# Two output projections of a decoder trunk, rewritten as one level of Strassen's scheme

## The chip, the cores and the metric

One core of a Trainium2 chip runs the whole kernel. The metric is the device time of one execution in microseconds (us). The kernel before has a median of 1701.39 us in three runs (1700.16 to 1702.24).

## The reference

A decoder trunk of two layers on 512 tokens of 2048 features, all in float32. Each layer computes `y`, multiplies it by an output weight of 2048 x 2048, and normalizes the sum with its input:

```
def even_layer(x, w_in, conv_w, cmp_pos, cmp_w1, cmp_w2, w_out, rel_table):
    ...
    return jnp.concatenate([y_a, y_b], axis=-1) @ w_out
def odd_layer(x, w_in, ln_g, ln_b, sgu_w, sgu_b, w_out):
    ...
    y = u * mixed.reshape(bsz, s, D_SGU) * jax.nn.silu(z)
    return y @ w_out
def reference(...):
    for layer in range(DEPTH):
        ...
        x = layer_norm(DEEPNORM_ALPHA * x + y, ln_g[layer], ln_b[layer])
    return x
```

The change concerns the two products with `w_out` and the additions and LayerNorms behind them.

## The kernel before

**Numbers.** A float32 product is made of three products of fp32r parts: `split` (lines 80 to 82) casts a tile to its high part on ScalarE and subtracts that from the tile on VectorE for the low part. Then hi·hi, lo·hi and hi·lo are added up in one PSUM bank. Weights pass through `split` in halves of 128x1024 (`whi`, `wlo`), from a raw buffer of 1 MB that SP's queue loads; activations are split once (`act_hi`, `act_lo`).

**Stages.** The even layer makes its features with feature-major units and attention heads and writes `y_sb` (features on partitions, 512 tokens). Output projection 1 multiplies by `wo0`. Its blocks are token-major: `proj_blocks` goes over column blocks of 512, 512, 512, 256 and 256 columns, `block_b` keeps one PSUM bank for each of the four row tiles of 128 tokens ("rows" below), and `mm_b` issues the three matmuls of one 128-deep piece (lines 113 to 115). In the last block each row is finished before the next row begins. `done0` loads the piece of x (`xs`), adds it to the bank into `xr`, and takes bn_stats; behind a row's last block `layer_norm` normalizes the row. VectorE does 1408 of its 2048 columns (lines 502 and 512), ScalarE and GpSimd the other 640 (lines 507 to 509), with the reciprocal root on GpSimd (line 498). `transposes0` (line 529) then turns row m-2 into `act_hi` and `act_lo`, and the last two rows are turned between the first blocks of the odd layer's projection (`wv1`).

**The odd layer** makes `v_sb` by that projection, then loops over 16 column tiles (units of `wuz`, the spatial mix into `pm`, line 601, and the gate, lines 597 to 607), and writes its `y` back into `v_sb`. Output projection 2 multiplies it by `wo1` in the same blocks; `done1` (line 614) adds, normalizes and stores rows.

**Order.** There is no table. A framework's scheduler orders each engine's instructions by the program's order and the buffers' dependences. SP issues the loads into one queue; each engine works through its own list in order.

## Time and profile before

| what | value |
|---|---|
| runs, median (lowest to highest) | 1701.39 us (1700.16 to 1702.24) |
| span of the profiled execution | 1699.9 us |
| TensorE busy | 1668.3 us, 98% |
| VectorE busy | 704.3 us, 41% |
| ScalarE busy | 464.1 us, 27% |
| GpSimd busy | 59.2 us, 3% |
| TensorE on the chain that ended last | 95% |
| mean granted clock of TensorE | 0.993 |

The span runs from the first to the last instruction of the profiled execution; no other time is listed for that execution, and the median of the runs is 1.5 us above it. The chain is followed back from the last instruction: a share of 95% says that TensorE waits for little. The busy time of matmuls overlaps, since their ends are modelled: what one matmul costs is read from the distance between two starts.

### The profile page before, as it was taken

The page shows a single profiled execution, that of the slowest core. Times are in us where ns is not written, and L with a number is a line of the kernel's source. Part 1 is how long each engine was busy: PE and PEld are TensorE (multiplying, and loading weights), DVE is VectorE, ACT ScalarE, POOL GpSimd, SP SyncE. Part 2 cuts the span into 40 slices and gives each one's busy share as a digit, 9 for nine tenths or more (in the row PEclk, how much of TensorE's full clock was granted, in tenths as well). Part 3 has the DMA queues.
Part 4 walks back from the last instruction along what each step waited for, and adds up shares of the span by engine and source line. Part 5 has one row for each costly group of instructions (what it writes and reads, how often), then busy time and mean ns, then how long its engine had stood idle before and what let it go on. Part 6 is the DMA issues. An engine that isn't in the chain of part 4 may idle for free.

```text
span 1699.9 us, 19851 instructions
## 1 busy us (share of the span) xinstructions
PE 1668.3 (98%) x8390; PEld 1423.9 (84%) x8390; DVE 704.3 (41%) x1161; ACT 464.1 (27%) x717; POOL 59.2 (3%) x96
## 2 busy tenths in 40 slices
PE   8999999999999999999999899999999999999995
PEld 6898888888988888888889898888888888888895
DVE  5225353444244435354334932233333333353337
ACT  4123232333232323243111422222222222241111
POOL 0100000000000000000000500000000000000004
PEclk9999999999999999999999999999999999999998
DMA  6542222222222222223334222222222222232222
GB/s 225 174 157 100 104 81 75 106 74 80 102 100 81 76 105 75 75 99 136 124 124 134 80 100 99 99 75 99 99 99 84 90 99 99 88 135 99 99 75 99
DMA packets 32244, 175.44 MB, mean 103 GB/s; under 512 B 4211, under 2 KB 7155, under 8 KB 13980
## 3 DMA queue, kind: packets, MB, share of 16 engines
q1 hardware_dynamic: 31340, 171.13, 28.4%
q0 software_dynamic: 672, 2.64, 0.5%
q8 instruction: 65, 1.06, 0.3%
q10 hardware_dynamic: 144, 0.41, 0.1%
q14 instruction: 23, 0.19, 0.0%
HBM read 169.95 MB, written 6.84 MB: 104 GB/s over the span
## 4 chain that ended last, share of the span: by engine, by line
PE 95%; DVE 2%; POOL 1%; issue 1%; DMA 0%; ACT 0%; SPq 0%; DVEq 0%; POOLq 0%
PE ps L106 18%; PE ps L104 18%; PE ps L105 18%; PE ps L115 11%; PE ps L114 11%; PE ps L113 11%; PE ps_t L377 1%; PE pm L601 1%; PE hp L271 1%; DVE xr L512 1%; PE po L320 1%; PE po L322 1%; PE po L321 1%; POOL rs L498 0%; PE ps_s L320 0%
## 5 line engine op out<-in xcount | busy, mean ns | idle before, releaser
L82 DVE TENSOR_TENSOR wlo<-raw,whi 128x1024 fp32r<-128x1024 f32 (+3 forms) x286 | 343.2, 1203 | 803.7 <-ACT whi L81 736.0
L81 ACT CAST whi<-raw 128x1024 fp32r<-128x1024 f32 (+3 forms) x286 | 295.0, 1035 | 1080.5 <-PE ps L105 575.5
L104 PE MATMUL ps<-act_hi,whi 128*128 128x512 f32 x1376 | 540.5, 393 | 0.0
L106 PE MATMUL ps<-act_hi,wlo 128*128 128x512 f32 x1376 | 536.0, 390 | 0.7 <-DVE wlo L82 0.7
L105 PE MATMUL ps<-act_lo,whi 128*128 128x512 f32 x1376 | 535.7, 389 | 0.0
L113 PE MATMUL ps<-whi,act_hi 128*128 128x512 f32 (+2 forms) x1088 | 371.0, 341 | 3.1 <-ACT act_hi L81 3.1
L114 PE MATMUL ps<-wlo,act_hi 128*128 128x512 f32 (+2 forms) x1088 | 370.7, 341 | 1.7 <-DVE wlo L82 1.7
L115 PE MATMUL ps<-whi,act_lo 128*128 128x512 f32 (+2 forms) x1088 | 370.6, 341 | 1.4 <-DVE act_lo L82 1.4
L106 PEld LDWEIGHTS ps<-act_hi,wlo 128*128 128x128 f32 x1376 | 258.3, 188 | 55.4 <-DVE wlo L82 1.1
L104 PEld LDWEIGHTS ps<-act_hi,whi 128*128 128x128 f32 x1376 | 258.5, 188 | 52.5 <-issue 0.7
L105 PEld LDWEIGHTS ps<-act_lo,whi 128*128 128x128 f32 x1376 | 258.5, 188 | 51.9 <-issue 0.2
L113 PEld LDWEIGHTS ps<-whi,act_hi 128*128 128x128 f32 x1088 | 207.0, 190 | 25.8 <-ACT act_hi L81 3.3
L114 PEld LDWEIGHTS ps<-wlo,act_hi 128*128 128x128 f32 x1088 | 206.9, 190 | 24.4 <-DVE wlo L82 2.0
L115 PEld LDWEIGHTS ps<-whi,act_lo 128*128 128x128 f32 x1088 | 206.8, 190 | 24.2 <-DVE act_lo L82 1.6
L358 ACT ACTIVATE t_sc<-t_sc,mx 128x128 f32<-128x128 f32 (+1 forms) x64 | 35.1, 550 | 17.0 <-DVE mx L355 17.0
L498 POOL TENSOR_TENSOR rs<-mv,epst 128x1 f32<-128x1 f32 x8 | 8.1, 1008 | 864.3 <-DVE mv L496 864.3
L82 DVE TENSOR_TENSOR p_lo<-ps_t,p_hi 128x512 fp32r<-128x512 f32 (+2 forms) x48 | 25.0, 549 | 0.5
L353 DVE CUSTOM_DVE_ANT_0 t_sc<-ps_s,bh 128x128 f32<-128x128 f32 (+3 forms) x56 | 24.3, 455 | 0.6
L507 ACT ACTIVATE xr<-xr,nm,rs 128x320 f32<-128x320 f32 (+1 forms) x15 | 9.2, 655 | 50.2 <-DVE nm L504 50.2
L364 DVE TENSOR_SCALAR t_sc<-t_sc,sm 128x128 f32<-128x128 f32 (+1 forms) x64 | 20.5, 382 | 0.6
L173 PE MATMUL ps<-act_hi,whi 128*128 128x512 f32 x32 | 13.9, 445 | 6.5 <-ACT act_hi L81 6.2
L377 PE MATMUL ps_t<-ident,t_sc 128*128 128x128 f32 x160 | 20.1, 273 | 0.0
(163 smaller groups left out, 881.9 us busy)
## 6 DMA issues: line engine op xcount, KB each, us to landing
raw<-in_wa_dram SPq DMA_DIRECT2D x54, 1024.0 KB, 4.8
raw<-in_wo_dram SPq DMA_DIRECT2D x32, 1024.0 KB, 4.8
raw<-in_wuz_dram SPq DMA_DIRECT2D x32, 1024.0 KB, 4.8
raw<-in_wv_dram SPq DMA_DIRECT2D x16, 1024.0 KB, 4.8
raw<-in_cw_dram SPq DMA_DIRECT2D x4, 1024.0 KB, 4.8
xraw<-in_xT_dram SPq DMA_DIRECT2D x7, 512.0 KB, 9.7
xs<-in_xn_dram SPq DMA_DIRECT2D x12, 256.0 KB, 3.4
raw<-in_wv_dram SPq DMA_DIRECT2D x4, 670.0 KB, 4.2
```

The source lines that it names most:

```text
L81: nc.scalar.copy(hi, src)
L82: nc.vector.tensor_tensor(lo, src, hi.bitcast(F32), ALU.subtract)
L104: nc.tensor.matmul(ps, hi[:, w], act_hi[:, kt, :], start=kt == 0, stop=False)
L105: nc.tensor.matmul(ps, hi[:, w], act_lo[:, kt, :], start=False, stop=False)
L106: nc.tensor.matmul(ps, lo[:, w], act_hi[:, kt, :], start=False, stop=kt == KT - 1)
L113: nc.tensor.matmul(ps[:, :width], act_hi[:, kt, ms], hi[:, w], start=kt == 0, stop=False)
L114: nc.tensor.matmul(ps[:, :width], act_hi[:, kt, ms], lo[:, w], start=False, stop=False)
L115: nc.tensor.matmul(ps[:, :width], act_lo[:, kt, ms], hi[:, w], start=False, stop=kt == KT - 1)
L353: nc.vector.tensor_tensor_reduce(out=t[:, offs[qb] + k0:offs[qb] + k1], in0=b[:, o:o + k1 - k0], in1=bh[:, BW - nk + k0:BW - nk + k1], sca ...
L358: nc.scalar.activation(t[:, offs[qb]:offs[qb] + nk], t[:, offs[qb]:offs[qb] + nk], AF.Exp, bias=mx[:, qb:qb + 1], accum_out=sm[:, qb:qb + 1])
L364: nc.vector.tensor_scalar(t[:, offs[qb]:offs[qb] + nk], t[:, offs[qb]:offs[qb] + nk], sm[:, qb:qb + 1], None, ALU.mult)
L377: nc.tensor.transpose(ps[:, i * P:(i + 1) * P], t[:, offs[qb] + kb * P:offs[qb] + (kb + 1) * P], ident)
```

## The change

Both projections become `strassen`. `y` and `w_out` are cut into halves by depth (k), by tokens (t) and, within each of two column groups of 1024 (g), by columns (n). Seven products of sums of quarters, in the order 1, 2, 5, 3, 7, 6, 4, take the place of eight. Each has 2 depth pieces (c) x 2 column groups x 2 row tiles x 4 depth tiles x 3 parts = 96 matmuls of 128x512, in units of 24 on one weight megabyte. The sums of activations are made by VectorE in `s_piece`. The sums of weights are made by DMAs: products 1 and 3 load four buffers `ch` of 1 MB each (SP, line 564), and for products 5, 7, 6 and 4 a DMA issued by GpSimd adds a further megabyte of the weight to the buffer (line 568), 16 of them in each projection. Product 2 uses the old raw buffers (line 561).

The sum over products is kept in `xr`: `stage` loads all of x into it (line 632, 4 x 1 MB) and the LayerNorm's gains and biases into `gb` (line 521, 2 x 1 MB) ahead of the weights, and each finished bank is added to one quarter by VectorE (line 581). Product 6 goes into all of three quarters by way of `ua`. Rows 0 and 1 are complete with product 6, rows 2 and 3 with product 4; `layer_norm` follows in each case. The scale of x is moved into `y` (YSCALE) and epsilon (LEPS). All transposes stand behind the first projection in the program. The pools change: `act_hi` and `act_lo` are given up before each projection and `ch` lies in their place; `xr` lies where tiles of the even layer lay, and the second `gb` where tiles of the odd layer's loop lay.

In the changed kernel `split` is at lines 86 and 87, the Strassen matmuls at lines 600 to 602, LayerNorm at lines 497 to 514, bn_stats at line 638 and the transposes at line 659.

```diff
+YSCALE = 0.5 / ALPHA
+LEPS = EPS / ALPHA ** 2
...
-BLOCKS = [(0, 512), (512, 512), (1024, 512), (1536, 256), (1792, 256)]
+BLOCKS = [(0, 512), (512, 512), (1024, 512), (1536, 512)]
...
-    act_hi = big.tile([P, KT, S], F32R, name="act_hi")
-    act_lo = big.tile([P, KT, S], F32R, name="act_lo")
+    act_hi = ea.tile([P, KT, S], F32R, name="act_hi")
+    act_lo = ea.tile([P, KT, S], F32R, name="act_lo")
...
-            nc.vector.scalar_tensor_tensor(y_sb[:, h, :], ah, 0.5, az, ALU.mult, ALU.mult)
+            nc.vector.scalar_tensor_tensor(y_sb[:, h, :], ah, YSCALE, az, ALU.mult, ALU.mult)
...
+    even.close()
+
+
+    xp = ctx.enter_context(tc.tile_pool(name="xp", bufs=1, side="right"))
     xr = xp.tile([P, NT, DM], F32, name="xr")
...
-    for kt in range(KT):
-        split(act_hi[:, kt, :], act_lo[:, kt, :], y_sb[:, kt, :])
...
+    def strassen(sp, w, y, half_done):
...
+        def a(k, t, c):
+            return y[:, 8 * k + 4 * c:8 * k + 4 * c + 4, t * 256:(t + 1) * 256]
+
+        def blk(k, n, g, c):
+            return w[4 * (2 * g + n) + 2 * k + c]
...
+        def s_piece(p, c):
+            if p == 5 and c == 0:
+                for d in range(2):
+                    f1[d] = sp.tile([P, 4, 256], F32, tag="f1", name="f1", bufs=2)
+                    nc.vector.tensor_tensor(f1[d], a(0, 1, d), a(1, 1, d), ALU.subtract)
+            if p == 3 and c == 0:
+                for d in range(2):
+                    nc.vector.tensor_tensor(a(0, 1, d), a(0, 0, d), a(0, 1, d), ALU.subtract)
+                    nc.vector.tensor_tensor(a(0, 0, d), f1[d], a(0, 0, d), ALU.subtract)
+                    nc.vector.tensor_tensor(a(1, 0, d), a(1, 0, d), a(0, 0, d), ALU.add)
+            src = {1: a(0, 0, c), 2: a(1, 0, c), 5: f1.get(c), 3: a(1, 0, c), 7: a(0, 1, c), 6: a(0, 0, c), 4: a(1, 1, c)}[p]
+            hi = sp.tile([P, 4, 256], F32R, tag="shi", name="shi", bufs=3)
+            lo = sp.tile([P, 4, 256], F32R, tag="slo", name="slo", bufs=3)
+            split(hi, lo, src)
+            return hi, lo
+
+        def t_parts(p, g, c):
+            if p == 2:
+                raw = wp.tile([P, 2048], F32, tag="raw", name="raw", bufs=2)
+                nc.sync.dma_start(raw, blk(1, 0, g, c))
+            elif p in (1, 3):
+                raw = chain[g, c] = sp.tile([P, 2048], F32, tag="ch", name="ch", bufs=4)
+                nc.sync.dma_start(raw, blk(0, 0, g, c) if p == 1 else blk(1, 1, g, c))
+            else:
+                raw = chain[g, c]
+                add = {5: (0, 1), 7: (0, 1), 6: (0, 0), 4: (1, 0)}[p]
+                nc.gpsimd.dma_start(raw, blk(*add, g, c), accum_op=ALU.add)
...
+                split(hi, lo, raw[:, d * 1024:(d + 1) * 1024])
...
+        for p in (1, 2, 5, 3, 7, 6, 4):
+            new = p in (1, 5, 7, 6)
+            for c in range(2):
+                shi, slo = s_piece(p, c)
+                for g in range(2):
+                    parts = t_parts(p, g, c)
+                    for m in range(2):
...
+                            nc.tensor.matmul(b, shi[:, k, ms], hi[:, ws], start=new and first, stop=False, **kw)
+                            nc.tensor.matmul(b, shi[:, k, ms], lo[:, ws], start=False, stop=False, **kw)
+                            nc.tensor.matmul(b, slo[:, k, ms], hi[:, ws], start=False, stop=last, **kw)
+                        if c == 0:
+                            continue
...
+                        elif p == 2:
+                            add(at(0, m, g, 0), b)
+                            half_done(m, 2 * g)
...
+                        elif p == 6:
+                            add(ua[g, m], b)
+                            add(at(0, m, g, 1), ua[g, m], ALU.subtract)
+                            half_done(m, 2 * g + 1)
+                            add(at(1, m, g, 1), ua[g, m], ALU.subtract)
+                            half_done(2 + m, 2 * g + 1)
+                            add(at(1, m, g, 0), ua[g, m])
+                        else:
+                            add(at(1, m, g, 0), b)
+                            half_done(2 + m, 2 * g)
+
+    def stage(sp, gbp, w, y, src, stats, g, finish):
+
+        if src is not None:
+            for m in range(NT):
+                nc.sync.dma_start(xr[:, m], src[m * P:(m + 1) * P])
+        gb = gbp.tile([P, 2, DM], F32, tag="gb", name="gb")
+        affine_rows(gb, g)
+        left = [4] * NT
+
+        def half_done(m, b):
+            nc.vector.bn_stats(stats[:, m, b], xr[:, m, b * 512:(b + 1) * 512])
+            left[m] -= 1
+            if not left[m]:
+                finish(m, gb)
+
+        strassen(sp, w, y, half_done)
...
+        stage(sp, gbp, wo0, y_sb, xn, stats0, 2, lambda m, gb: layer_norm(xr, gb, stats0, m, LNS))
...
-    proj_blocks(wo0, BLOCKS, done0)
+    for m in range(NT):
+        transposes0(m)
...
-        vdone.append((m, b))
-        if len(vdone) < 3:
-            transposes0(NT - 3 + len(vdone))
...
-    proj_blocks(wo1, BLOCKS, done1)
...
+        stage(sp, gbp, wo1, v_sb.rearrange("p k n c -> p k (n c)"), None, stats1, 0, out_rows)

```

**SP at the start of projection 1.** SP's queue before (raw is a weight megabyte, xs a piece of x, gb the gains and biases):

```order
L87 DMA raw<-in_wa_dram 128x2048 x11
L87 DMA raw<-in_wo_dram 128x2048 x4
L534 DMA xs<-in_xn_dram 128x512 x2
L519 DMA gb_5692<-in_odg_dram 128x2048 x2
L87 DMA raw<-in_wo_dram 128x2048 x3
L534 DMA xs<-in_xn_dram 128x512 x4
```

The same place now (xr is all of x, ch a weight megabyte of product 1):

```order
L92 DMA raw<-in_wa_dram 128x2048 x11
L561 DMA raw<-in_wo_dram 128x2048 x2
L632 DMA xr<-in_xn_dram 128x2048 x4
L521 DMA gb<-in_odg_dram 128x2048 x2
L564 DMA ch<-in_wo_dram 128x2048 x4
L561 DMA raw<-in_wo_dram 128x2048 x2
L92 DMA raw<-in_wv_dram 128x2048 x2
```

Before, four weight megabytes were issued ahead of x and the gains; now two megabytes of product 2 are, and six megabytes (xr and gb) stand ahead of the first weight of product 1. In the second projection there is no xr, and two megabytes (gb) stand ahead.

**VectorE where the first LayerNorm begins.** Before, in the last block of projection 1 (wlo is the low part of a weight, xr the rows):

```order
L82 TENSOR_TENSOR wlo<-raw,whi 128x1024
L539 SCALAR_TENSOR_TENSOR xr<-xs,ps 128x256
L540 BN_STATS stats_5687<-xr 128x6
L495 BN_AGGR mv<-stats_5687 128x2
L496 TENSOR_SCALAR mv<-mv 128x1
L502 SCALAR_TENSOR_TENSOR xr<-xr,mv,gb_5692 128x512
L504 TENSOR_SCALAR nm<-mv,rs 128x1
L502 SCALAR_TENSOR_TENSOR xr<-xr,mv,gb_5692 128x512
L502 SCALAR_TENSOR_TENSOR xr<-xr,mv,gb_5692 128x384
L512 SCALAR_TENSOR_TENSOR xr<-xr,rs,gb_5692 128x512 x2
L512 SCALAR_TENSOR_TENSOR xr<-xr,rs,gb_5692 128x384
```

Now, from the end of product 6 (ua is a bank of product 6, the first wlo the first half weight of product 4):

```order
L581 TENSOR_TENSOR ua<-ua,ps 128x512
L87 TENSOR_TENSOR wlo<-ch,whi 128x1024
L581 TENSOR_TENSOR xr<-xr,ua 128x512 x2
L638 BN_STATS stats_5656<-xr 128x6 x2
L581 TENSOR_TENSOR xr<-xr,ua 128x512
L581 TENSOR_TENSOR ua<-ua,ps 128x512 x2
L581 TENSOR_TENSOR xr<-xr,ua 128x512 x2
L638 BN_STATS stats_5656<-xr 128x6 x2
```

and on, after the LayerNorm of row 0 and the statistics of row 1:

```order
L581 TENSOR_TENSOR xr<-xr,ua 128x512
L498 TENSOR_SCALAR mv<-mv 128x1
L504 SCALAR_TENSOR_TENSOR xr<-xr,mv,gb 128x512
L506 TENSOR_SCALAR nm<-mv,rs 128x1
L504 SCALAR_TENSOR_TENSOR xr<-xr,mv,gb 128x512
L504 SCALAR_TENSOR_TENSOR xr<-xr,mv,gb 128x384
L514 SCALAR_TENSOR_TENSOR xr<-xr,rs,gb 128x512 x2
L514 SCALAR_TENSOR_TENSOR xr<-xr,rs,gb 128x384
L87 TENSOR_TENSOR wlo<-ch,whi 128x1024 x7
```

Before, the low part of the weight stood ahead of a row's LayerNorm, and one row followed. Now product 4's first half weight stands early, and the other seven behind all of product 6's additions and the LayerNorms of rows 0 and 1. In the second projection VectorE's list is the same at this place.

**TensorE at the same place** (product 4's matmuls, lines 600 to 602; line 659 are the transposes of row 0):

```order
L600 MATMUL ps<-whi,shi 128x512
L601 MATMUL ps<-wlo,shi 128x512
L602 MATMUL ps<-whi,slo 128x512
L600 MATMUL ps<-whi,shi 128x512 x3
L659 MATMUL ps_x<-ident,xr 128x128 x16
L601 MATMUL ps<-wlo,shi 128x512
L602 MATMUL ps<-whi,slo 128x512
L600 MATMUL ps<-whi,shi 128x512
```

Of product 4 16 matmuls stand ahead of the transposes of row 0, and the next (L601) uses the first of the seven late wlo. The other 48 transposes, of rows 1 to 3, stand behind product 4 and ahead of the first matmul of `wv1`; before, those of the last two rows stood between the blocks of `wv1`.

## Rows read from the trace of the kernel before

**Rows 1.** The page: the span; busy time, share and instructions of TensorE.

```profile
span 1699.9 us, 19851 instructions
PE 1668.3 (98%) x8390; PEld 1423.9 (84%) x8390; DVE 704.3 (41%) x1161; ACT 464.1 (27%) x717; POOL 59.2 (3%) x96
```

**Rows 2.** Groups by line and shape: the projections' matmuls (out<-in xcount | busy, mean ns | idle before).

```profile
L113 PE MATMUL ps<-whi,act_hi 128*128 128x512 f32 x576 | 224.3, 389 | 0.0
...
L113 PE MATMUL ps<-whi,act_hi 128*128 128x256 f32 x384 | 110.0, 286 | 3.1 <-ACT act_hi L81 3.1
```

**Rows 3.** Timeline of PE at the start of the second projection: start, duration.

```profile
1505.52 0.48 PE L113 MATMUL ps<-whi,act_hi 128*128 128x512 f32 x1
1505.83 0.40 PE L114 MATMUL ps<-wlo,act_hi 128*128 128x512 f32 x1
...
1508.79 0.39 PE L115 MATMUL ps<-whi,act_lo 128*128 128x512 f32 x1
```

**Rows 4.** Timeline of PE in a 256-wide block of the first projection.

```profile
924.62 0.28 PE L113 MATMUL ps<-whi,act_hi 128*128 128x256 f32 x1
...
925.46 0.28 PE L114 MATMUL ps<-wlo,act_hi 128*128 128x256 f32 x1
```

**Rows 5.** Busy time by stretch, at the first LayerNorm: window, span, engines, PEclk, DMA share, GB/s.

```profile
950.00:960.00 10.00, 5.17 (x32) 4.67 (x31) 10.00 (x15) 6.46 (x10) 4.67 (x4) 0.76 0.06 7
960.00:968.00 8.00, 6.57 (x49) 6.36 (x48) 7.56 (x12) 3.21 (x6) 5.69 (x5) 0.88 0.30 125
```

**Rows 6.** The chain of waits: start-up, start of projection 1, transposes.

```profile
12.79 0.54 PE ps L174
...
16.69 0.24 PE ps L175
...
771.87 0.24 PE ps L113
...
968.94 0.55 PE ps_x L529 x5
```

**Rows 7.** Timeline of DVE: the last operation of the even layer.

```profile
773.43 0.68 DVE L469 SCALAR_TENSOR_TENSOR y_sb<-ah,az 128x512 f32<-128x512 f32 x1
```

**Rows 8.** Busy time by stretch, at the start, with the DMA queue full.

```profile
10.00:15.00 5.00, 3.54 (x10) 2.15 (x9) 4.28 (x4) 3.90 (x4) 0.00 (x0) 0.81 1.03 417
20.00:25.00 5.00, 5.00 (x24) 4.14 (x23) 3.79 (x4) 2.24 (x3) 0.00 (x0) 1.00 0.96 370
```

**Rows 9.** DMA issues: operation, xcount, KB each, us from issue to landing.

```profile
raw<-in_wo_dram SPq DMA_DIRECT2D x32, 1024.0 KB, 4.8
...
rscr<-rrow POOLq DMA_DIRECT2D x8, 320.0 KB, 8.4
...
gb<-in_odg_dram SPq DMA_DIRECT2D x2, 1024.0 KB, 8.6
```

**Rows 10.** Groups by line and shape: VectorE and ScalarE operations that return in the changed kernel.

```profile
L82 DVE TENSOR_TENSOR wlo<-raw,whi 128x1024 fp32r<-128x1024 f32 x270 | 329.8, 1224 | 756.2 <-ACT whi L81 688.4 <-PE pm L601 63.1 <-PE ps_t L377 4.2
L81 ACT CAST whi<-raw 128x1024 fp32r<-128x1024 f32 x270 | 283.2, 1052 | 1032.9 <-PE ps L105 556.7 <-PE ps L115 358.2 <-issue 66.6
...
L607 DVE TENSOR_TENSOR v_sb<-ug,th 128x512 f32<-128x512 f32 x16 | 11.1, 692 | 0.6
...
L82 DVE TENSOR_TENSOR act_lo<-ps_x,act_hi 128x512 fp32r<-128x512 f32 x16 | 10.0, 670 | 0.1
...
L617 DVE SCALAR_TENSOR_TENSOR xr<-xr,ps 128x512 f32<-128x512 f32 x12 | 7.9, 680 | 0.4
...
L618 DVE BATCH_NORM_STATS2 stats<-xr 128x6 f32<-128x512 f32 x12 | 7.7, 682 | 0.0
```

**Rows 11.** Timeline of DVE: LayerNorm of row 2 in the second projection, then row 3.

```profile
1681.16 0.29 DVE L495 BATCH_NORM_AGGREGATE mv<-stats 128x2 f32<-128x30 f32 x1
...
1687.73 0.41 DVE L617 SCALAR_TENSOR_TENSOR xr<-xr,ps 128x256 f32<-128x256 f32 x1
```

**Rows 12.** Timeline of ACT at the end of the odd layer's loop.

```profile
1505.70 0.59 ACT L597 ACTIVATE th<-ps 128x512 f32<-128x512 f32 x1
```

More of the change, by code (lines that the diff above doesn't have):

```diff
@@ L70, in trunk @@
     wp = ctx.enter_context(tc.tile_pool(name="wp", bufs=2))
+    even = ExitStack()
+    ea = even.enter_context(tc.tile_pool(name="ea", bufs=1))
     psp = ctx.enter_context(tc.tile_pool(name="psp", bufs=8, space=PS))
@@ L519, in affine_rows, with at, add @@
             nc.sync.dma_start(gb[:, i], odg[g + i:g + i + 1].to_broadcast([P, DM]))
-    gb0 = lp.tile([P, 2, DM], F32, name="gb0", bufs=1)
+    def strassen(sp, w, y, half_done):
[3 more added lines that the diff above has]
+            return w[4 * (2 * g + n) + 2 * k + c]
+        f1 = {}
+        chain = {}
+        ua = {}
+        def s_piece(p, c):
[24 more added lines that the diff above has]
+                nc.gpsimd.dma_start(raw, blk(*add, g, c), accum_op=ALU.add)
+            parts = []
+            for d in range(2):
+                hi = wp.tile([P, 1024], F32R, tag="hi", name="whi", bufs=4)
+                lo = wp.tile([P, 1024], F32R, tag="lo", name="wlo", bufs=4)
+                split(hi, lo, raw[:, d * 1024:(d + 1) * 1024])
+                parts.append((hi, lo))
+            return parts
+        def at(t, m, g, n):
+            return xr[:, 2 * t + m, (2 * g + n) * 512:(2 * g + n + 1) * 512]
+        def add(dst, src, op=ALU.add):
+            nc.vector.tensor_tensor(dst, dst, src, op)
+        banks = {}
+        for p in (1, 2, 5, 3, 7, 6, 4):
[5 more added lines that the diff above has]
+                    for m in range(2):
+                        if new and c == 0:
+                            banks[g, m, p] = bank()
+                        b = banks[g, m, {2: 1, 3: 5, 4: 7}.get(p, p)]
+                        ms = slice(m * P, m * P + P)
+                        for k in range(4):
+                            hi, lo = parts[k // 2]
+                            ws = slice(k % 2 * 512, k % 2 * 512 + 512)
+                            first, last = c == 0 and k == 0, c == 1 and k == 3
+                            kw = {} if new else {"skip_group_check": True}
+                            nc.tensor.matmul(b, shi[:, k, ms], hi[:, ws], start=new and first, stop=False, **kw)
[3 more added lines that the diff above has]
+                            continue
+                        if p == 1:
+                            ua[g, m] = sp.tile([P, 512], F32, tag="ua", name="ua", bufs=4)
+                            nc.scalar.copy(ua[g, m], b)
+                        elif p == 2:
+                            add(at(0, m, g, 0), b)
+                            half_done(m, 2 * g)
+                        elif p == 5:
+                            add(at(1, m, g, 1), b)
+                        elif p == 3:
+                            add(at(0, m, g, 1), b)
+                        elif p == 7:
+                            add(at(1, m, g, 1), b, ALU.subtract)
+                        elif p == 6:
[8 more added lines that the diff above has]
+                            half_done(2 + m, 2 * g)
@@ L607, in trunk, with out_rows @@
             nc.vector.tensor_tensor(v_sb[:, j].rearrange("p n c -> p (n c)"), ug, th, ALU.mult)
-    for kt in range(KT):
-        split(act_hi[:, kt, :], act_lo[:, kt, :], v_sb[:, kt].rearrange("p n c -> p (n c)"))
-    gl = big.tile([P, 2, DM], F32, tag="big0", name="gl")
-    def done1(m, c0, width, ps):
-        b = BLOCKS.index((c0, width))
-        dst = xr[:, m, c0:c0 + width]
-        nc.vector.scalar_tensor_tensor(dst, dst, ALPHA, ps[:, :width], ALU.mult, ALU.add)
-        nc.vector.bn_stats(stats1[:, m, b], dst)
-        if b == 1 and m == 0:
-            affine_rows(gl, 0)
-        if c0 + width == DM:
-            layer_norm(xr, gl, stats1, m, LNE if m == NT - 1 else LNS, lambda n, cs: (nc.scalar if n % 2 and m == NT - 1 else nc.sync).dma_start(out[m * P:(m + 1) * P, cs], xr[:, m, cs]))
-    proj_blocks(wo1, BLOCKS, done1)
+    odd.close()
+    def out_rows(m, gb):
+        layer_norm(xr, gb, stats1, m, LNE if m == NT - 1 else LNS, lambda n, cs: (nc.scalar if n % 2 and m == NT - 1 else nc.sync).dma_start(out[m * P:(m + 1) * P, cs], xr[:, m, cs]))
+    with tc.tile_pool(name="sp1", bufs=1) as sp, tc.tile_pool(name="gb1", bufs=1, side="right") as gbp:
+        stage(sp, gbp, wo1, v_sb.rearrange("p k n c -> p k (n c)"), None, stats1, 0, out_rows)
 def t5_bucket(n):
```

35 lines of the change are left out of this document (11 added, 24 removed).

## The prediction

> **What bounds the kernel now.** I read the page first: TensorE is busy 1668.3 of 1699.9 us [rows 1], and nearly the whole chain that ended last lies on it. So a matmul taken away is worth its distance to the next, and any wait that is put in front of TensorE costs its full length. Next I read the groups by line and shape for the number of matmuls, and TensorE's timeline for their distance. The mean of 389 ns in the group [rows 2] is a modelled length and overlaps the next matmul; the starts are the measure. In the second projection 14 starts run from 1505.83 to 1508.79 [rows 3]: 2.96 / 13 = 0.228 us for a matmul of 512 columns. In a 256-wide block 8 starts run from 924.62 to 925.46 [rows 4]: 0.84 / 7 = 0.120 us. Then I looked for stretches in which TensorE does wait, since the change could close or open such holes. The one large hole is the first LayerNorm: in 950 to 968 us TensorE is busy 5.17 + 6.57 of 18 us [rows 5], so 6.3 us are idle there. The starts of both projections have no hole: the first matmul of projection 1 is on the chain at 771.87 [rows 6], that of projection 2 starts at 1505.52 [rows 3].
>
> **What the change takes away.** Line 113 has 576 matmuls of 512 and 384 of 256 columns [rows 2] for three projections, so one projection has, over its three lines, 576 and 384 too: 576 x 0.228 + 384 x 0.120 = 177.4 us. Now it has 7 x 96 = 672 of 512 columns: 153.2 us. That is **-24.2 us each, -48.4 together**. The old hole goes too, **-6.3**, and with it one restart of the clock. What a restart costs is seen at the start of the kernel: after its wait TensorE's granted clock is 0.81 in 10 to 15 us [rows 8], and the nine distances from 12.79 to 16.69 [rows 6] take 3.90 us in place of 9 x 0.228 = 2.05: 1.8 us lost while the clock goes from its lower level to 2.4 GHz. At the old hole the clock fell to 0.76 [rows 5], so I take **-1.8**.
>
> **The start of projection 1.** The first weight of product 1 is the seventh megabyte in SP's queue, behind four of xr and two of gb, and xr's memory was the even layer's, so its loads wait for the last y_sb, which ends at 773.43 + 0.68 = 774.1 [rows 7]. Before, the weights were loaded ahead and xs and gb beside the matmuls. Seven times 1.05 MB is 7.34 MB. With a full queue the core moved 417 and 370 GB/s [rows 8]; at 400 that is 18.4 us. A lone megabyte takes 4.8 us from issue to landing [rows 9], of which 2.6 are transfer at that rate, so 2.2 are a start. Then ScalarE casts the first half, 1.05 us [rows 10]. So 774.1 + 2.2 + 18.4 + 1.1 = 795.8, against a TensorE that is done with the even layer at 771.9: **+23.9**. The two megabytes of product 2 that were prefetched don't help, since product 1 comes first. Bounds: 417 or 370 GB/s give 17.6 or 19.8 us of transfer; a gb megabyte took 8.6 us [rows 9], and if two of them cost that each, 12 us more.
>
> **From product 6 to product 4.** VectorE now has, from the end of the first bank of product 6 to the second half weight of product 4: four additions to ua at 0.68, twelve to xr at 0.69, eight bn_stats at 0.68, two low parts at 1.22 [rows 10], and the LayerNorms of rows 0 and 1. One LayerNorm with its aggregation takes VectorE from 1681.16 to 1687.73 [rows 11], 6.57 us, a wait for GpSimd included. The sum is 2.7 + 8.3 + 5.5 + 2.4 + 13.1 = 32.0 us. The first bank is ready 36 matmuls (8.2 us) before the end of product 6, so that half weight is ready 23.8 us after it. TensorE has 16 matmuls, 3.6 us, in front of the one that needs it: it is idle for 20.2 us. In projection 1 the 16 transposes of row 0 lie in this time; five take 0.55 us [rows 6], so 1.8: **+18.4** there. In projection 2 the order is the same without transposes: **+20.2**. Before, a half weight was split ahead of a row's LayerNorm, and one row followed at a time.
>
> **From product 4 to the odd layer.** The first matmul of wv1 stands behind the 48 transposes of rows 1 to 3, which want LayerNorm row 3 and free banks. Product 4's last bank of row 2 is ready 12 matmuls (2.7 us) before its end. VectorE adds and takes statistics (1.4) and does row 2 (6.57): 5.2 us after the end. Then come row 3's addition and statistics (1.4), three splits of transposed rows (2.0) [rows 10] and row 3's LayerNorm: 15.2 us. Some seven of the 13 splits left, at 0.67, then free the banks for the last transposes: 19.9 us, of which 48 x 0.11 = 5.3 are transposes that were there before: **+14.6**. The two weight splits for wv1 stand behind all 13, so I add **+1** for a second short wait.
>
> **The start of projection 2.** Its gb takes memory of the odd layer's loop and waits for the last gate. TensorE ends the loop at 1505.5 [rows 3]; one activation (0.59 [rows 12]) and four VectorE operations of 0.69 [rows 10] later, at about 1508.9, SP may issue. Three megabytes at 400 GB/s take 7.9 us, with 2.2 and 1.1 around them: 1520.1, so **+14.6**.
>
> **Restarts and the end.** Five new holes of over 10 us bring five restarts at 1.8: **+9.0**. At the end the last addition and statistics work on 512 in place of 256 columns: **+0.5**.
>
> **Edits at nothing.** GpSimd's 32 DMA issues stand on an engine that was busy 59.2 us [rows 1]. VectorE's sums of activations and low parts come to some 22 us in the fullest of the middle products (eight low parts of weights, two of activations, six sums at 1.22 and four additions at 0.68: 22.2), about the 96 x 0.228 = 21.9 us of TensorE beside them; with the lighter products around it that costs under 1 us.
>
> **The weight sums.** No row of before shows an accumulating DMA. It is hidden as long as a megabyte takes no more than the 24 matmuls on it, 5.47 us. From below it is a plain copy, 2.6 us at the full rate; from above I take the row of GpSimd's own queue, 8.4 us from issue to landing [rows 9], as the time of one megabyte. A gain is excluded, as the copy alone is needed at least. I take it as hidden, since the queue rows of a weight megabyte (4.8, of which a part is start) are nearest in size. The Trainium skill, "Collectives: The Full Stack", section "The bandwidth ceiling: the fold count and why AG ≠ RS ≠ AR", says that a DMA that adds reads two sources, with two read descriptors for each chunk on one ring, and so runs at half the rate of a copy; as an estimate by that, two times 2.6 is 5.2 us, under 5.47 by little, and at 370 GB/s it would be 5.7, which adds 24 x 0.2 = 5 us. No run here shows it yet.
>
> **The sum.** -48.4 - 6.3 - 1.8 + 23.9 + 18.4 + 20.2 + 14.6 + 1 + 14.6 + 9.0 + 0.5 = +45.7 us on the span of 1699.9. The median of the runs is 1.5 above the span, so the same on it: **1747 us**, slower by 2.7%.
>
> **The rivals.**
> - *The weight sums fall behind.* For it: 4 in 7 products hang on them, one after another on one queue, each on the buffer of the sum before. Against it: they can start a product early. It decides from 5.47 us per megabyte. At 8.4 us, 12 sums in each projection (the first four have a product's time in hand) lose 2.9 each: 2 x 12 x 2.9 = 70 us, 1817.
> - *VectorE does not hold TensorE*, and the change is **faster**. The place is between products 6 and 4 and behind 4. For it: VectorE is busy 41% on the whole, so it might start these additions early and finish them in time. It decides when the 32.0 us of work are under 8.2 + 3.6 = 11.8. Then 18.4, 20.2, 14.6, 1 and three restarts (5.4) go: 45.7 - 59.6 = -13.9, so 1687. Against it: the order on VectorE is fixed, and the durations are rows.
> - *The starts cost nothing*, because the loads of xr and gb are early or give way to the first weight. Then 23.9, 14.6 and two restarts go: +3.6, so 1705. Against it: the loads stand ahead in SP's one queue, and xr's memory is not free earlier.
> - That the change doesn't make seven products is out: the lists have 672 matmuls a projection.
>
> **How the numbers follow.** The forecast gets 0.66, the weight sums 0.22, the free VectorE 0.06 and the free starts 0.06. The forecast's own range is 1730 (restarts at nothing, VectorE's work a tenth shorter) to 1771 (both gb loads slow, 24 us). The range reaches on into the case of slow sums, to 1810, and down to 1715 for a start that is half hidden. A measurement of this kernel can tell about 0.2%, 3.4 us, from no change. Faster: the free VectorE and a little of the free starts, 0.07. Same: most of the rest of the free starts, 0.04. Slower: 0.89.
>
> **What would show it.** Right: TensorE's line in 40 slices has holes at about 772 to 796, near product 4 of both projections, and at the start of projection 2; the chain of waits has VectorE's LayerNorm lines (504, 514) and SP's loads of xr, gb or ch on it; the granted clock is down behind each hole; matmuls of lines 600 to 602 keep 0.228 us. Wrong: a chain through the DMAs of line 568 and low parts that wait for ch inside products 5, 7 and 6 would be the first rival; product 4 without a hole the second; a first Strassen matmul near 775 the third.

## The result, and the profile after

The changed kernel takes **1745.32 us** (median of 4 runs, 1744.46 to 1746.27) against 1701.51 for the kernel before: a ratio of 1.0258, 95% interval 1.0243 to 1.0272. It is slower by 44 us; forecast were 1747 us and 45.7 more on the span, which grew by 42.6, from 1699.9 to 1742.5.

The page of the kernel after, first its span and TensorE (against [rows 1]), then the two queues, DMAs issued by SP (q1) and by GpSimd (q0):

```profile
span 1742.5 us, 18922 instructions
PE 1634.3 (94%) x7814; PEld 1376.6 (79%) x7814; DVE 813.8 (47%) x1245; ACT 528.3 (30%) x769; POOL 86.5 (5%) x128
...
q1 hardware_dynamic: 27884, 162.74, 26.0%
q0 software_dynamic: 5280, 36.20, 10.4%
```

TensorE is busy 34 us less and the span is 42.6 longer, so it waits some 77 us more. What it waited for, in the two projections (engine, line, what it waited for: us in total, times, longest), first from 765 to 1010 us:

```profile
PE ps L600 <- ACT whi L86: 21.9, 1, 21.9
PE ps L601 <- DVE wlo L87: 9.4, 2, 9.0
PE ps_x L659 <- DVE xr L514: 6.7, 2, 5.4
PE ps_x L659 <- DVE xr L581: 5.2, 1, 5.2
PE ps_x L659 <- DVE act_lo L87: 5.0, 1, 5.0
```

and from 1500 to 1742:

```profile
PE ps L601 <- DVE wlo L87: 20.4, 2, 19.6
PE ps L600 <- ACT whi L86: 13.7, 1, 13.7
```

The waits in these two tables come to 82.3 us, and the kernel before has 6.2 there, so they hold the 77 us: ScalarE's cast of the first weight (21.9 and 13.7) is the two starts; VectorE's low part of a weight (9.4 and 20.4, of which 9.0 and 19.6 are product 4's) is the step from product 6 to product 4; the transposes (ps_x) wait for VectorE in the middle of product 4 (6.7) and behind it (5.2 and 5.0). The holes in TensorE's timeline that belong to them: start and duration of the instruction behind each hole, in brackets the hole's length and what ended it. Two rows without brackets are the first transposes behind product 4 and the first matmul of the odd layer:

```profile
793.77 1.19 PE L600 MATMUL ps<-whi,shi 128*128 128x512 f32 x2 [21.87 <-ACT whi L86]
...
936.45 1.11 PE L659 MATMUL ps_x<-ident,xr 128*128 128x128 f32 x4 [5.39 <-DVE xr L514]
...
938.85 2.82 PE L659 MATMUL ps_x<-ident,xr 128*128 128x128 f32 x12 [1.29 <-DVE xr L514]
...
950.65 0.79 PE L601 MATMUL ps<-wlo,shi 128*128 128x512 f32 x1 [8.98 <-DVE wlo L87]
...
970.83 1.47 PE L659 MATMUL ps_x<-ident,xr 128*128 128x128 f32 x12
...
977.49 3.83 PE L659 MATMUL ps_x<-ident,xr 128*128 128x128 f32 x16 [5.19 <-DVE xr L581]
...
986.31 4.50 PE L659 MATMUL ps_x<-ident,xr 128*128 128x128 f32 x20 [4.99 <-DVE act_lo L87]
...
990.46 0.56 PE L118 MATMUL ps<-whi,act_hi 128*128 128x256 f32 x1
...
1546.33 1.22 PE L600 MATMUL ps<-whi,shi 128*128 128x512 f32 x2 [13.73 <-ACT whi L86]
...
1703.67 0.79 PE L601 MATMUL ps<-wlo,shi 128*128 128x512 f32 x1 [19.58 <-DVE wlo L87]
```

And the windows of the kernel after at the first start, inside products 3 to 6, and in the hole (the columns as in [rows 5]):

```profile
775.00:785.00 10.00, 0.00 (x0) 0.00 (x0) 9.27 (x9) 0.82 (x1) 0.00 (x0) 0.50 1.00 422
875.00:885.00 10.00, 10.00 (x46) 8.29 (x45) 6.86 (x9) 4.45 (x5) 1.72 (x2) 1.00 1.03 202
935.00:945.00 10.00, 3.94 (x16) 3.14 (x16) 9.55 (x15) 1.19 (x3) 5.64 (x6) 0.50 0.00 0
```

At the start the DMA engines are full and move 422 GB/s. Inside the products they are full again (share 1.03) but move only 202 GB/s: the adding DMAs take their time. In the hole VectorE is busy 9.55 of 10 us and GpSimd 5.64 with its share of LayerNorm; TensorE does no more than row 0's 16 transposes (3.94 us), and its granted clock is 0.50, the lower level of 1.2 GHz.

### The profile page after: what moved, and what is told of

Read it like the earlier page. It is cut to its first block, busy times and chain, and to the rows that moved or that the text cites. A ratio compares the mean times of both kernels' runs of the same rounds, so it can differ in the third digit from the quotient of the medians.

```text
span 1742.5 us, 18922 instructions
## 1 busy us (share of the span) xinstructions
PE 1634.3 (94%) x7814; PEld 1376.6 (79%) x7814; DVE 813.8 (47%) x1245; ACT 528.3 (30%) x769; POOL 86.5 (5%) x128
## 3 DMA queue, kind: packets, MB, share of 16 engines
q0 software_dynamic: 5280, 36.20, 10.4%
## 4 chain that ended last, share of the span: by engine, by line
PE 89%; DVE 5%; issue 2%; DMA 2%; POOL 1%; ACT 1%; SPq 0%; DVEq 0%; POOLq 0%; ACTq 0%
PE ps L111 18%; PE ps L109 18%; PE ps L110 18%; PE ps L601 5%; PE ps L602 5%; PE ps L600 5%; PE ps L120 4%; PE ps L119 4%; PE ps L118 4%; DVE xr L514 1%; PE ps_t L382 1%; DMA ch<-in_wo_dram 1%; PE hp L276 1%; PE pm L712 1%; DMA raw<-in_wo_dram 1%
## 5 line engine op out<-in xcount | busy, mean ns | idle before, releaser
L87 DVE TENSOR_TENSOR wlo<-raw,whi 128x1024 fp32r<-128x1024 f32 (+2 forms) x238 | 284.4, 1199 | 624.9 <-ACT whi L86 557.3
L86 ACT CAST whi<-raw 128x1024 fp32r<-128x1024 f32 (+2 forms) x238 | 244.7, 1031 | 843.5 <-PE ps L110 561.9
L600 PE MATMUL ps<-whi,shi 128*128 128x512 f32 x448 | 176.3, 397 | 35.6 <-ACT whi L86 35.6
L601 PE MATMUL ps<-wlo,shi 128*128 128x512 f32 x448 | 178.6, 399 | 29.8 <-DVE wlo L87 29.8
L602 PE MATMUL ps<-whi,slo 128*128 128x512 f32 x448 | 177.6, 396 | 0.0
L118 PE MATMUL ps<-whi,act_hi 128*128 128x512 f32 (+2 forms) x448 | 148.2, 331 | 0.0
L120 PE MATMUL ps<-whi,act_lo 128*128 128x512 f32 (+2 forms) x448 | 148.2, 331 | 0.0
L119 PE MATMUL ps<-wlo,act_hi 128*128 128x512 f32 (+2 forms) x448 | 148.2, 331 | 0.0
L601 PEld LDWEIGHTS ps<-wlo,shi 128*128 128x128 f32 x448 | 86.3, 193 | 50.6 <-DVE wlo L87 32.5
L118 PEld LDWEIGHTS ps<-whi,act_hi 128*128 128x128 f32 x448 | 85.2, 190 | 7.5
L120 PEld LDWEIGHTS ps<-whi,act_lo 128*128 128x128 f32 x448 | 85.1, 190 | 7.4
```

Of the source, the lines that this page charges most:

```text
L86: nc.scalar.copy(hi, src)
L87: nc.vector.tensor_tensor(lo, src, hi.bitcast(F32), ALU.subtract)
L118: nc.tensor.matmul(ps[:, :width], act_hi[:, kt, ms], hi[:, w], start=kt == 0, stop=False)
L119: nc.tensor.matmul(ps[:, :width], act_hi[:, kt, ms], lo[:, w], start=False, stop=False)
L120: nc.tensor.matmul(ps[:, :width], act_lo[:, kt, ms], hi[:, w], start=False, stop=kt == KT - 1)
L600: nc.tensor.matmul(b, shi[:, k, ms], hi[:, ws], start=new and first, stop=False, **kw)
```

## The experiments

**1. Weights first.** The loads of xr and gb are issued behind product 1's weights.

```diff
                     parts = t_parts(p, g, c)
+                    if p == 1 and c == 1 and g == 1:
+                        loads()
...
-        if src is not None:
-            for m in range(NT):
-                nc.sync.dma_start(xr[:, m], src[m * P:(m + 1) * P])
...
-        affine_rows(gb, g)
```

> In both projections the loads of xr and gb are issued behind the four weight megabytes of product 1 instead of ahead of them; nothing else changes. If the start holes come from SP's queue order, the first weight of projection 1 lands one lone-megabyte time (4.8 us) after the issue at about 773 us, so the hole of 21.9 us shrinks to about 7 (15 us less). In projection 2 the weight lands 5 us earlier, but VectorE has eight of its own operations ahead of the first low part, so only 4 us are gained there. Sum: 1745.3 - 19 = 1726 us (1722 to 1731). Rival: the DMA engines are full in products 1 to 6 anyway (share 0.9 to 1.0), and the six megabytes now collide with the adding DMAs; then most of the gain is lost again inside products 2 and 5, where new waits on ch appear, and the time stays above 1738.

Measured: 1737.91 us (1737.21 to 1738.43), 7.4 less than the changed kernel. TensorE's holes at the first start and in product 2, and SP's issues there:

```profile
778.57 1.19 PE L602 MATMUL ps<-whi,shi 128*128 128x512 f32 x2 [6.85 <-ACT whi L86]
...
824.65 0.80 PE L602 MATMUL ps<-whi,shi 128*128 128x512 f32 x1 [10.12 <-ACT whi L86]
```

```profile
772.67 2.12 SPq L564 DMA_DIRECT2D ch<-in_wo_dram  x4
774.84 1.98 SPq L637 DMA_DIRECT2D xr<-in_xn_dram  x4
777.42 2.94 SPq L521 DMA_DIRECT2D gb<-in_odg_dram  x2
801.07 6.49 SPq L561 DMA_DIRECT2D raw<-in_wo_dram  x2
```

The start hole fell from 21.9 to 6.9 us, as expected, so SP's queue order is its cause. But a hole of 10.1 us opened in product 2: its third raw megabyte is issued at 801 us behind what is left of the 6 MB, beside the first adding DMAs, and lands 22.4 us later. In projection 2, where only gb is moved, 8.8 us are left of 13.7. On the whole the rival came out (above 1738), and not the 1726 expected: most of what the start gained was lost again in product 2.

**2. LayerNorm behind product 4.** Rows 0 and 1 are normalized when row 2 is complete; their LayerNorm is so written behind product 4's splits.

```diff
             if not left[m]:
-                finish(m, gb)
+                if m < 2:
+                    ready.append(m)
+                else:
+                    flush()
+                    finish(m, gb)
...
+        def flush():
+            while ready:
+                finish(ready.pop(0), gb)
```

> The LayerNorms of rows 0 and 1 are written behind product 4 in the program, so VectorE splits product 4's weights before them; nothing else changes. If VectorE's order holds TensorE between products 6 and 4, the 13 us of LayerNorm leave that place and the holes there shrink from 15.7 and 19.6 us to about 8 each. But VectorE is busy nearly all the time from there to the odd layer, so a part comes back behind product 4, where row 2's addition queues behind the moved LayerNorms. Sum over both projections: 14 to 20 us less, about 1728 us. Rival: TensorE is held by something else there (the sum of weights or ScalarE's casts), then the holes stay and the time is 1743 to 1747.

Measured: 1724.00 us, 21.3 less, a little more than expected. The holes behind product 6 and behind product 4, and the one in projection 2:

```profile
934.82 0.80 PE L601 MATMUL ps<-wlo,shi 128*128 128x512 f32 x1 [5.56 <-DVE wlo L87]
...
959.50 0.65 PE L669 MATMUL ps_x<-ident,xr 128*128 128x128 f32 x4 [1.21 <-DVE xr L581]
...
968.17 1.97 PE L669 MATMUL ps_x<-ident,xr 128*128 128x128 f32 x8 [8.01 <-DVE act_lo L87]
...
975.70 4.93 PE L669 MATMUL ps_x<-ident,xr 128*128 128x128 f32 x24 [5.57 <-DVE act_lo L87]
...
1679.59 0.79 PE L601 MATMUL ps<-wlo,shi 128*128 128x512 f32 x1 [5.56 <-DVE wlo L87]
```

VectorE's order does hold TensorE there: 9.0 + 6.7 us became 5.6, and 19.6 became 5.6. That is 24.1 us (9.0 + 6.7 - 5.6, and 19.6 - 5.6). Two places take some of it back. The transposes behind product 4 wait 1.2 + 8.0 + 5.6 us in place of 5.2 + 5.0, which is 4.6. And in projection 2 the moved LayerNorms put off the last rows: from TensorE's last matmul to the end of the span it is 21.3 us here (1699.3 to 1720.6) and 18.2 in the changed kernel (1724.3 to 1742.5), which is 3.1. Some 3 us are gained besides, because row 0's transposes no longer run at the lower clock in the hole. That makes some 19 of the 21.9 us between the two spans; 1.5 more lie ahead of projection 1, where nothing was changed. The even layer, which no edit touches, ends between 769.9 and 771.8 us in these traces, so a difference of 2 us between two executions says nothing.

**3. Plain loads for the sums.** The DMAs copy and don't add (the sums of weights are left out).

```diff
-                nc.gpsimd.dma_start(raw, blk(*add, g, c), accum_op=ALU.add)
+                nc.gpsimd.dma_start(raw, blk(*add, g, c))
```

> The DMAs of the weight sums are issued in the same place by the same engine, but copy in place of adding (the sums of weights are left out, so products 5, 7, 6 and 4 use single quarters). If the adding is hidden, the time is the same, 1745 us within 3, and only the DMA share inside products 5 to 6 falls, from 0.9 to 1.0 to about 0.55. Rival: the weight sums hold TensorE somewhere or slow other engines; then it is over 5 us faster, up to the 70 us of the prediction's rival.

Measured: 1741.90 us, 3.4 less, ratio to before 1.0235 (1.0220 to 1.0251), which overlaps that of the changed kernel. Of TensorE's holes one of 0.5 us in product 2 is gone, and the others are the same within 0.2. The rows of the same DMAs, copying:

```profile
q0 software_dynamic: 5280, 36.20, 5.9%
...
ch<-in_wo_dram POOLq DMA_DIRECT2D x32, 1024.0 KB, 5.0
```

GpSimd's queue in the kernel before, and the row of the DMAs in the changed kernel, adding:

```profile
q0 software_dynamic: 672, 2.64, 0.5%
```

```profile
ch<-in_wo_dram POOLq DMA_DIRECT2D x32, 1024.0 KB, 10.0
```

The 32 DMAs of 1.05 MB are hidden, adding or copying. But they differ in price: with the bytes the same, q0's share is 5.9% here and 10.4% when they add. Before it was 0.5% without them, so one megabyte takes 5.4% of 1740 us / 32 = 2.9 us of all 16 engines as a copy, and 9.9% of 1742.5 / 32 = **5.4 us as an addition** (at the 202 GB/s of the window above, 5.2), and 10.0 us from issue to landing in place of 5.0.

**4. Transposes as before.** Those of rows 2 and 3 stand between the odd layer's first blocks again.

```diff
-    for m in range(NT):
+    for m in range(2):
         transposes0(m)
...
+        vdone.append((m, b))
+        if len(vdone) < 3:
+            transposes0(NT - 3 + len(vdone))
```

> The transposes of rows 2 and 3 stand between the first blocks of the odd layer's projection again, as in the kernel before; those of rows 0 and 1 stay ahead. If the transposes in front of the odd layer cost what the prediction's step says, the 10.2 us of holes behind product 4 fall to some 6, as before: 4 to 8 us less, 1737 to 1741. Rival: VectorE's list, which still has LayerNorm of row 3 ahead of row 0's last split, sets the first matmul of the odd layer; then 0 to 4 us.

Measured: 1741.63 us, 3.7 less: in the rival's range (0 to 4), just short of the 4 to 8 expected. Of 5.2 + 5.0 us of holes behind product 4, 5.2 + 2.9 are left. The odd layer's first matmul now starts at 977.8 us in place of 990.5, so row 3's LayerNorm, which VectorE ends at 985.7, does not set it. But row 1's last four transposes still wait until VectorE has added product 4's last bank (5.2), behind row 2's LayerNorm, and row 2's last eight for a split behind row 3's LayerNorm (2.9).

**5. Every sum twice.** (The second summand is added twice.)

```diff
                 nc.gpsimd.dma_start(raw, blk(*add, g, c), accum_op=ALU.add)
+                nc.gpsimd.dma_start(raw, blk(*add, g, c), accum_op=ALU.add)
```

> Each adding DMA of the changed kernel is issued twice (so the sums contain the second summand twice). If a megabyte that is added fills the DMA engines for about 5.3 us (share 0.97 in products 3 to 6, at 188 GB/s) against 5.47 us of matmuls on it, there is no room: each doubled sum costs some 5 us, 12 of them in each projection, so about 120 us more, 1865 us (1845 to 1900). Rival: the engines only wait on something in those rows and have room; then less than 40 us more.

Measured: 1830.57 us, 85 more, between the two expectations. TensorE's waits in the first projection:

```profile
PE ps L601 <- ACT whi L86: 59.3, 7, 21.9
PE ps_x L660 <- DVE xr L582: 6.7, 1, 6.7
PE ps_x L660 <- DVE act_lo L87: 5.0, 1, 5.0
PE ps L602 <- DVE wlo L87: 3.3, 7, 0.8
```

Of these 59.3 us 21.9 are the old start; the rest are new waits for weights, most of them some 6 us, at every second megabyte. Over that stretch the DMA engines are full:

```profile
900.00:920.00 20.00, 13.15 (x49) 9.73 (x50) 6.47 (x7) 4.95 (x6) 3.52 (x4) 0.84 1.02 208
```

At 208 GB/s a megabyte that is added takes 5.0 us. So there is no room for a second one: a sum just fits into its 5.47 us of matmuls, and twice that does not. The cost is below the 120 expected, which counted the 12 sums of products 7, 6 and 4 without a start: the first sum of product 7 is issued at 864.5 us, 22 us ahead of its first matmul (886.6).

**6. Product 2 first.** Its first two megabytes lie in their raw buffers before the even layer ends; it gets banks of its own, and xr and gb are loaded behind product 1's weights.

```diff
-        for p in (1, 2, 5, 3, 7, 6, 4):
-            new = p in (1, 5, 7, 6)
+        for p in (2, 1, 5, 3, 7, 6, 4):
+            new = p in (1, 2, 5, 7, 6)
...
-                        b = banks[g, m, {2: 1, 3: 5, 4: 7}.get(p, p)]
+                        b = banks[g, m, {3: 5, 4: 7}.get(p, p)]
```

> Product 2, whose first two weight megabytes are already in their raw buffers, comes ahead of product 1, with banks of its own that are added to xr when product 1 ends; the loads of xr and gb stand behind the weights of product 1. In the run with weights first the start hole shrank but a hole of 10 us opened in product 2, because its third megabyte stood behind xr and gb. If that is the whole of it, both go here: the holes at the starts fall from 21.9 and 14.5 us to some 5 each (the split of the activations), nothing opens later, and the time is 1745.3 - 17 - 9 = about 1719 us (1715 to 1725). Rival: the DMA engines are short of time around the start in any order; then a hole of 5 to 10 us opens at product 5 or 1 and the time is 1728 or more.

Measured: 1714.76 us, 30.6 less, better than expected. The start holes are 3.6 and 5.3 us, in which TensorE waits for ScalarE's split of the activations, and nothing opens later. Behind the first of them the clock did not fall: it is 1.00 from 774 to 780 us.

**7. Three edits together** (2, 4 and 6).

> The edits of three runs together: product 2 first, the LayerNorms of rows 0 and 1 behind product 4's splits, and the transposes of rows 2 and 3 between the odd layer's blocks. If the holes are independent, their gains add up: 26 + 21.3 + 3.7 = 51 less than 1745.3, 1694 us (1688 to 1700), faster than the kernel before. Rival: VectorE's work is the bound between products 6 and the odd layer, so that the moved LayerNorm and the moved transposes share one gain; then 1700 or more, no better than before.

Measured: 1695.28 us, ratio to before 0.9963 (0.9948 to 0.9978). The gains add up to 55.6, and 50.0 were measured. That LayerNorm and transposes share a gain, as the rival has it, does not show in the trace: behind product 4 the holes are 0.3 + 8.0 + 3.6 = 11.9 us, where the holes of the changed kernel with both differences would be 10.2 + 4.6 - 2.1 = 12.7. Some 2.5 us are a restart at the first start: its hole is 3.6 us as in experiment 6, but the granted clock is 0.53 from 774 to 780 us here, and the matmuls start 0.43 us apart until 781. The rest stays open.

**8. GpSimd adds.** As 7, with eight of product 6's twelve additions on GpSimd and the last half of product 4 row by row.

```diff
-                            add(at(1, m, g, 1), ua[g, m], ALU.subtract)
-                            half_done(2 + m, 2 * g + 1)
-                            add(at(1, m, g, 0), ua[g, m])
+                            nc.gpsimd.tensor_tensor(at(1, m, g, 0), at(1, m, g, 0), ua[g, m], ALU.add)
+                            nc.gpsimd.tensor_tensor(at(1, m, g, 1), at(1, m, g, 1), ua[g, m], ALU.subtract)
```

> As the three edits together, and GpSimd does eight of the twelve additions of product 6 to xr (those to rows 2 and 3), and the last half of product 4 goes row by row (row 2 complete 24 matmuls before the end in place of 12). If VectorE's backlog is what is left of the holes between products 6 and 4 (5.6 us in each projection), they close: 2 x 5.6 and two restarts of 2 us, and row 2's earlier end gives up to 2.7 in each projection; some 15 to 20 us less than the three edits together, about 1677 us. Rival: GpSimd's additions are slow (1.8 us each by its 320-column rows) and slow VectorE's own two-input operations beside them; then no gain, or a few us slower than the three edits.

Measured: 1693.65 us, the same as 7 (the ranges overlap). From first to last matmul the projections got 3.2 and 2.5 us shorter, but the end behind the last matmul grew from 20.2 to 24.6 us; which of the two edits did what was not separated. The groups of the additions on the two engines, and then VectorE's in experiment 7:

```profile
L630 POOL TENSOR_TENSOR xr<-xr,ua 128x512 f32<-128x512 f32 x8 | 15.9, 1984 | 1.9 <-DVE ua L581 1.8
...
L631 POOL TENSOR_TENSOR xr<-xr,ua 128x512 f32<-128x512 f32 x8 | 14.2, 1774 | 0.0
...
L581 DVE TENSOR_TENSOR xr<-xr,ua 128x512 f32<-128x512 f32 x8 | 9.8, 1229 | 0.1
```

```profile
L581 DVE TENSOR_TENSOR xr<-xr,ua 128x512 f32<-128x512 f32 x24 | 15.5, 681 | 0.1
```

The rival holds: VectorE's addition of two SBUF tiles takes 1229 ns beside GpSimd's, against 681 where GpSimd adds nothing. The Trainium skill, "SBUF — State Buffer", section "Who interferes with whom", says that a VectorE instruction with two inputs in SBUF contends with a GpSimd instruction that reads SBUF; these rows agree.

**9. LayerNorm on VectorE alone** (edit of the changed kernel: `LNS` and `LNE` give all 2048 columns to VectorE).

```diff
-LNS = ([(0, 512), (512, 1024), (1024, 1408)], [(1408, 1728), (1728, 2048)])
+LNS = ([(0, 512), (512, 1024), (1024, 1536), (1536, 2048)], [])
```

> The changed kernel with the whole of each LayerNorm's two passes on VectorE (2048 columns in pieces of 512), in place of 1408 columns there and 640 on ScalarE and GpSimd. In the runs so far VectorE's second pass takes 1.25 us per 512 columns while GpSimd works, and 0.61 for the one piece that ran while GpSimd was idle. If GpSimd's work is what slows it, a row takes about 5.5 us in place of 6.6 although VectorE does 45% more columns, and the time falls by 4 to 6 us, to about 1740. Rival: the second pass is slow of itself; then a row takes over 8 us and the time is 1750 or more.

Measured: 1739.99 us, 5.3 less. The second pass (line 514) of the changed kernel, and then of this run:

```profile
L514 DVE SCALAR_TENSOR_TENSOR xr<-xr,rs,gb 128x512 f32<-128x512 f32 x14 | 17.7, 1303 | 0.0
```

```profile
L514 DVE SCALAR_TENSOR_TENSOR xr<-xr,rs,gb 128x512 f32<-128x512 f32 x32 | 21.9, 747 | 0.0
```

With GpSimd idle it takes 747 ns in place of 1303: the help of GpSimd cost VectorE as much time as it took off it. Over the whole kernel VectorE is busy 809.8 us in place of 813.8, with 45% more columns of LayerNorm. ScalarE's share went too, but it is not the cause: in the changed kernel VectorE's second pass of row 0 takes 3.75 us from 935.0, while GpSimd works until 939.5 and ScalarE ended its part at 935.2. The holes between products 6 and 4 shrink from 15.7 and 19.6 us to 13.9 and 17.8, the end behind the last matmul from 18.2 to 16.9.

**10. The same in the kernel before.**

> The kernel before the change with the whole LayerNorm on VectorE, nothing else: what the LayerNorm edit alone is worth without Strassen's scheme. Its hole of 6.3 us hangs on three rows of LayerNorm in a row, about 1 us less for each, and the last row at the end 1 to 2 less: 1696 us (1693 to 1699). Rival: the shares were balanced, then 1700 or more.

Measured: 1701.94 us, ratio 1.0004 (0.9996 to 1.0013): no difference, as the rival has it. The holes at the first LayerNorms come to 8.1 us (0.6 + 1.9 + 4.3 + 1.4) in place of 6.3, and the end behind the last matmul to 15.9 in place of 17.8: the one eats the other.

**11. VectorE's order rewritten.** As 7, with 9, weights split one unit ahead, product 6's additions to rows 2 and 3 put off to product 4, the LayerNorms of rows 0 and 1 ahead of them, the last half of product 4 row by row, and row 3's first LayerNorm behind the transposes of rows 0 and 1. One of these edits:

```diff
                 elif p == 6:
                     add(ua[g, m], b)
                     add(at(0, m, g, 1), ua[g, m], ALU.subtract)
                     half_done(m, 2 * g + 1)
-                    add(at(1, m, g, 1), ua[g, m], ALU.subtract)
-                    half_done(2 + m, 2 * g + 1)
-                    add(at(1, m, g, 0), ua[g, m])
                 else:
+                    add(at(1, m, g, 1), ua[g, m], ALU.subtract)
+                    half_done(2 + m, 2 * g + 1)
+                    add(at(1, m, g, 0), ua[g, m])
                     add(at(1, m, g, 0), b)
```

> The three edits together, and five more on VectorE's order: weights are split one unit ahead; of product 6's additions those to rows 2 and 3 stand behind product 4's splits; LayerNorm of rows 0 and 1 before them; the last half of product 4 row by row; row 3's LayerNorm of the first projection behind the transposes of rows 0 and 1; and all of LayerNorm on VectorE. If VectorE's backlog is the rest of the loss, the holes of 5.6 us in both projections close (with a restart of 2 us each: 15 us), the hole of 8 us ahead of the odd layer falls to some 2, and LayerNorm gives 4: some 15 to 22 us less than the 1695.3 of the three edits, about 1677 us (1670 to 1685). Rival: VectorE's work is conserved and it is the bound from product 6 to the odd layer in any order; then 1688 or more.

Measured: **1687.69 us** (1686.88 to 1688.55), ratio to before **0.9921** (0.9907 to 0.9934): faster than both kernels. TensorE's waits from 890 to 980 us, and VectorE's busy time in the windows behind product 6 and at the end:

```profile
PE ps_x L694 <- DVE xr L581: 13.3, 3, 8.0
PE ps_x L694 <- DVE xr L514: 1.5, 2, 0.9
PE ps L119 <- DVE wlo L87: 1.1, 1, 1.1
```

```profile
905.00:915.00 10.00, 10.00 (x46) 8.29 (x45) 9.98 (x14) 4.23 (x4) 0.00 (x0) 1.00 0.20 41
935.00:945.00 10.00, 1.55 (x7) 0.75 (x5) 9.56 (x18) 0.00 (x0) 0.99 (x1) 0.50 0.00 0
1660.00:1670.00 10.00, 0.00 (x0) 0.00 (x0) 9.56 (x19) 0.00 (x0) 0.92 (x1) 0.51 0.05 17
```

The holes between products 6 and 4 are closed, and against experiment 7 each projection is 9.6 us shorter from its first to its last matmul. But 4.3 us came back between the projections, where the transposes now wait 13.3 us for additions to xr, and 8.2 at the end: TensorE's last matmul starts at 1657.25, VectorE works on until 1681.9, and the span ends at 1685.6. From 905 to 965 and from 1640 to 1680 us VectorE is busy at least 9.3 of every 10. The expected 1677 was missed on the side of the rival (1688 or more): in this order VectorE's work is the bound. That no other order does better was not shown.

## Why the prediction was right

The time, the sign and the causes came out, and no term is off by more than 2 us. One of them is right by luck, as said below.

| step | forecast | measured in the trace after |
|---|---|---|
| matmuls, old hole, old restart | -56.5 | not read by itself; 42.6 less the rows below leaves -55.3 |
| start of projection 1 | +23.9 | 21.9 |
| product 6 to 4, projection 1 | +18.4 | 17.8: holes of 15.7 (5.4 + 1.3 + 9.0), and 16 transposes in 3.9 us, priced at 1.8 |
| product 6 to 4, projection 2 | +20.2 | 19.6 |
| product 4 to the odd layer | +14.6 and +1 | 14.3 (970.8 to 990.5, less the 5.3 of 48 transposes) and 0 |
| start of projection 2 | +14.6 | 14.5 (13.7 + 0.8) |
| restarts | +9.0 | 9.3: 3.8 and 4.6 in the projections, 0.9 in the odd layer's first matmuls |
| end | +0.5 | 0.5 |

The restarts are what the 672 matmuls of a projection take beyond the 153.2 us priced, from first to last without holes and transposes: 157.0 and 157.8.

- **The starts.** SP issued xr at 772.9 and the first ch at 776.0; it landed 16.6 us later. SP was 1.2 us earlier than the 774.1 assumed, and the queue moved 422 GB/s against 400, which is 1.0: together the 2 us. Experiments 1 and 6 show the cause: what stands ahead in the queue. In projection 2 one thing was not foreseen: VectorE computes seven sums and three low parts of activations while it waits, and these hold the first low part of a weight by another 0.8 us.
- **Product 6 to 4.** VectorE's chain ran from 919.7 to 949.9, 30.2 us against 32.0 summed, mainly since operations in a row start 0.60 apart and not their listed 0.68. The first of it, and the row whose first of four instructions (some 1.3 us) releases TensorE, in the trace after:

```profile
919.72 0.68 DVE L581 TENSOR_TENSOR ua<-ua,ps 128x512 f32<-128x512 f32 x1
...
948.72 5.28 DVE L87 TENSOR_TENSOR wlo<-ch,whi 128x1024 fp32r<-128x1024 f32 x4
```

  Experiments 2 and 11 take the LayerNorms, then the additions, out of this place, and the hole goes from 19.6 to 5.6 to none.
- **Product 4 to the odd layer.** The first matmul of wv1 starts 19.6 us behind product 4, and 19.9 were forecast, but the last part went another way. Row 3's LayerNorm ended 14.7 us behind product 4 (15.2 forecast). Then not seven splits of 4.7 us in all came first, but a single one; behind it the last 20 transposes run one after another from 986.31 to 990.46. That is 0.21 us each at a granted clock of 0.50, where 0.11 was priced [rows 6]. The path was wrong there, and that 4.7 us and the time of a split with 20 slow transposes come to the same is luck. It is also why the holes (5.2 + 5.0) are smaller than the term: TensorE is busy in the rest of it with transposes at the lower clock.
- **The weight sums** were hidden, as forecast, but the reason given (nearest in size to a loaded megabyte) was not the right one. The price is 5.2 to 5.4 us of full DMA engines, some 1.8 times a copy, and it fits by 0.1 to 0.3 us. The estimate of 5.2 in the prediction was the better one. It was worked out from the Trainium skill, "Collectives: The Full Stack", section "The bandwidth ceiling: the fold count and why AG ≠ RS ≠ AR", where a reduction reads two sources for each chunk and so runs at half the rate of a copy. The trace agrees with the rate (202 against 422 GB/s); no run here shows that two reads are the reason.
- **The other side.** The rival that VectorE does not hold TensorE is refuted by experiment 2, the one of free starts by 1 and 6. With the loads and VectorE's work in another order, the scheme does gain: experiment 11 is 57.6 us below the changed kernel and 13.8 below the one before, of the 48.4 us at which the removed matmuls were priced.

## What to carry to other kernels

Where TensorE is busy 98% of the time, matmuls taken away are paid only if what replaces them also hides: list for every other engine the work that the new scheme puts between two stages, and ask whether the next stage's first operand is queued behind it. Put the operand that starts a stage ahead of everything that is needed later, in the queue as on the engine, and look afterwards at the next place where the moved transfer or operation is awaited. Work given to GpSimd beside VectorE's two-input operations may give nothing.
